# Two-layer hybrid trunk on one core: the attention bias loaded from POOL's queue, the weighted sums' finish marked urgent, and two tiles of the output projection in a pair of PSUM banks

## The chip, the cores and the metric

The kernel runs on one core of a Trainium2 chip. The metric is the device time of one execution in microseconds (us). Before the change it is 1185.64 us, the median of three runs (1185.47 to 1185.81).

## The reference

The program is a two-layer trunk over 256 latent tokens and 256 context tokens of width 1024. Each layer has a gated feed-forward block, a mixer and a second feed-forward block, each behind an RMS norm that is scaled and shifted by vectors made from the conditioning. Layer 0's mixer holds the code in question. It is an attention with 8 heads of 64, beside four pooling groups, and one output projection over both:

```python
q, k, v, u = jnp.split(hl @ w_in, [NA_WIDTH, 2 * NA_WIDTH, 3 * NA_WIDTH], axis=-1)
...
bias = rpb[:, ri[:, None, :, None], ci[None, :, None, :]]
s_win = jnp.einsum('brqhd,brkwhd->bhrqkw', qg, k_blk) * scale + bias
s_win = jnp.where(col_ok[:, None, :], s_win, NEG_INF)
...
p = jax.nn.softmax(jnp.concatenate([s_win, s_ctx], axis=-1), axis=-1)
o = einsum(p_win, v_blk) + einsum(p[..., n_win:], v_ctx)
...
pool = multiscale_pool(u, pool_w, pool_scale)
y_lat = jnp.concatenate([att, pool], axis=-1) @ w_out
```

So a query sees the keys of its grid window, with a bias out of a small table and a mask on the columns, and all context keys. Layer 1's mixer is a short gated convolution that ends in an output projection of the same form, `W_out(B * conv3(C * x_in))`.

## The kernel before

**Data.** Every weight and activation is split into a high and a low part, and a product is made of three matmuls (`mm3`, L250) or of two (`mm2`, L256), whose first takes high and low of the activation side by side as 512 columns. Weights come from memory in order of use as one stream (`Stream`, L66): SP loads a `raw` tile of two chunks (L90), ACT makes the high part `whi` (L102), DVE the low part `wlo` (L103). Three chunks are split ahead of use, in four buffers.

**Order.** The tile framework schedules the first stage by hand and the rest by its own planner, which takes instructions by priority (`tc.high_priority(offset=URGENT)` raises it) and fixes one order for each engine. On the chip every engine goes through its order without overtaking. SP, and POOL too, are such queues: an instruction that waits, a DMA issue as well, holds up all that stands behind it.

**PSUM.** There are two kinds of buffers: three pairs of banks (`pair`, L135) and two single banks (`single`, L138). A new pair takes the place of the one that was handed out three pairs before, and waits for that one's last reader; a single, of the one two singles before.

**The mixer of layer 0** (`even_mixer`, L627) goes through four turns i, each for two heads. A turn has: `v_turn` (L737), where TensorE (PE) turns the values over (`pvt`); `scores` (L746), where PE makes scores `ps`, `top` (L762) adds the bias to them on DVE (`sm`, L766) and takes the maximum (`st`, L771), and `power` (L773) makes the exponential on ACT (L776); then, for the next turn, the projections of queries, keys and values (`pq`, `pk`, `pv`) with their finishing steps `tq`, `tk`, `tv` on DVE, which read PSUM and so free its banks; `turn` (L782), the transposes of the probabilities `pT`; `weigh` (L794), the weighted sums `po`; and `weigh_finish` (L808), whose four steps on ACT and DVE write the result into `m2` (`mh`, `ml`). Ahead of the turns come the projections for the pooling groups, `pu`, read by DVE (`tu`, L611) and written to `u` (L669). POOL makes the running means `s`, `pd` out of `u` (`pool_means`, L674), and `pool_map` (L692) multiplies them in turn 1 (`pp`, L695, finished on ACT and DVE, L699 and L700).

**The bias.** `load_bias(i)` (L640) fills a tile of 128x1024 elements from the table by 8 DMAs of 64 KB, each 64 partitions by 4 rows of 64 elements. There are two buffers, so the load for turn i+2 waits until turn i's scores have read theirs. `bias_mask` (L652) then puts a large negative number at the masked columns, on DVE (L654). Before the change SP issues these DMAs, in one queue with the weights.

**The output projection** (`OutProj`, L898) makes eight tiles d of 128 output columns, each of eight blocks k. For layer 0 tiles 0 to 3 are begun early, without block 3, which is the last to be ready; `rest` (L921) adds that block to them and then makes tiles 4 to 7 whole, each in a single bank. Layer 1 has three early tiles, and 3 to 7 are made whole. Each finished tile goes to `residual` (L600; two steps on DVE at L603, for both halves of its 512 columns) and to the next norm's `feed` (L360; ACT L368 and L372, DVE L369 and L374).

Of the kernel before, what the change touches and what calls it, by code (L numbers as in the profile page):

```python
# [9 lines left out]
F32 = mybir.dt.float32  # L10
# [4 lines left out]
ALU = mybir.AluOpType  # L15
# [14 lines left out]
GW = 64  # L30
# [6 lines left out]
URGENT = 400  # L37
# [82 lines left out]
def hybrid_trunk_kernel(ctx: ExitStack, tc: tile.TileContext, xc, cols_d, modw, wst, poolw_d,  # L120
                        rpb, notok_d, rcnt_d, out):
    nc = tc.nc
# [12 lines left out]
    def pair(name):  # L135
        return ps2.tile([P, 2, 512], F32, tag="pair", name=name)

    def single(name):  # L138
        return ps1.tile([P, 512], F32, tag="single", name=name)
# [487 lines left out]
    def even_mixer(act):  # L627
        with tc.tile_pool(name="mix", bufs=2) as ap_:
            m2 = ap_.tile([P, KD, 2, T], F32R, name="m2", bufs=1)
            mh, ml = m2[:, :, 0, :], m2[:, :, 1, :]  # L630
# [9 lines left out]
            def load_bias(i):  # L640
                b = ap_.tile([P, 2, 2, 4, GW], F32, tag="bias", name=f"bias{i}")
                for r in range(4):
                    for h in range(2):
                        src = bass.AP(
                            rpb.tensor,
                            rpb.offset + (2 * i + h) * RPB_R * RPB_C + (7 - r) * RPB_C - 48,
                            [[1, GW], [RPB_C, 4], [1, GW]],
                        )
                        nc.sync.dma_start(b[(r % 2) * GW : (r % 2) * GW + GW, r // 2, h], src)
                return b  # L650

            def bias_mask(b):  # L652
# [155 lines left out]
            def weigh_finish(i, pt):  # L808
                t = ap_.tile([P, 544], F32, tag="t", name=f"to{i}", bufs=2)
                o, r = t[:, 0:256], t[:, 256:512]  # L810
                nc.scalar.copy(r, pt[:, 1, 0:256])
                nc.vector.tensor_tensor(o, pt[:, 0, 0:256], r, ALU.mult)
                nc.scalar.copy(mh[:, i, :], o)
                nc.vector.tensor_tensor(ml[:, i, :], o, mh[:, i, :].bitcast(F32), ALU.subtract)


            wq, wk = W.get(), W.get()
# [8 lines left out]
            held["v", 0] = [pv0[:, q, 0:258] for q in range(2)]  # L826
            rr.root()
            bias = {0: load_bias(0)}
            project_u(0)
            rr.spread()  # L830
# [17 lines left out]
            for i in range(4):  # L848
                v = v_turn(i)
                if i + 1 < 4:  # L850
                    bias[i + 1] = load_bias(i + 1)
                pr, top, power, parts = scores(i, bias[i])
                if i + 1 < 4:
# [17 lines left out]
                    po = weigh(i, tn, v, parts)  # L871
                    v_finish(i + 1)
                    weigh_finish(i, po)
                    bias_mask(bias[i + 1])
                    if i == 1:
                        pool_map()
                else:
# [13 lines left out]
                    proj_out.early(2)  # L891
                    po = weigh(i, tn, v, parts)
                    weigh_finish(i, po)
                    proj_out.early(3)
                    proj_out.rest()
            return a2

    class OutProj:  # L898
# [22 lines left out]
        def rest(self):  # L921
            for d in range(self.n):
                self.block(d, self.late, False, True)
                self.done(d)
            for d in range(self.n, KD):
                self.pts[d] = single(f"pwo{self.l}{d}")
                for k in range(KD):
                    self.block(d, k, k == 0, k == KD - 1)
                self.done(d)
# [136 lines left out]
    with tc.tile_pool(name="g1", bufs=1) as gp:  # L1066
# [6 lines left out]
        for a, b in ((0, 1), (1, 2), (2, 4), (4, 6), (6, 8)):  # L1073
            o = done[:, a:b, :]
# [128 lines left out]
```

## Time and profile before

The profiled execution took 1185.92 us, 0.28 us above the median; its first to its last instruction span 1184.1 us.

| what | us |
|---|---|
| median of the runs | 1185.64 |
| profiled execution | 1185.92 |
| its span | 1184.1 |
| PE busy (97% of the span) | 1154.5 |
| DVE busy (78%) | 928.4 |
| ACT busy (48%) | 573.9 |
| POOL busy (2%) | 21.1 |

How to read it: PE is the engine that is nearly always at work; the clock granted to it is 0.99 of full speed on the mean. A stretch in which another engine idles means little. What counts is an instruction for which PE waits, and then what that instruction had waited for. A row of a timeline has the start, the duration, the engine, the line, the operation, its output and inputs, the count, and in brackets the idle time ahead of it with what ended it. The mixer of layer 0 lies between 393 and 520 us of the span.

### The profile page before, as it was taken

How to read it: one execution, taken by the hardware profiler on the slowest of the kernel's cores; microseconds unless marked ns; L12 is line 12 of the kernel's file. 1: busy time of each engine (PE TensorE's matmuls, PEld its weight loads, DVE VectorE, ACT ScalarE, POOL GpSimd, SP SyncE). 2: the span in 40 equal slices, each digit the busy share in tenths (PEclk: the TensorE clock that was granted, in tenths of full speed). 3: DMA queues.
4: the chain of work that ended last, by engine and by line, in shares of the span. 5: the costliest groups of instructions: out<-in, count | busy, mean ns of one | idle time of the engine just before them, and what ended most of it. 6: DMA issues, size and time to landing. Idle time of an engine off the chain costs nothing.

```text
span 1184.1 us, 16775 instructions
## 1 busy us (share of the span) xinstructions
PE 1154.5 (97%) x6570; PEld 990.4 (84%) x6570; DVE 928.4 (78%) x1486; ACT 573.9 (48%) x890; POOL 21.1 (2%) x23
## 2 busy tenths in 40 slices
PE   4999999999999999999999999999999999999997
PEld 2568888888888987889888889888889989988886
DVE  8977686577788586788898998788998888766663
ACT  4353221223234445567556447555546656655642
POOL 2000000000000040000000000000000000000000
PEclk7999999999999999999999999999999999999998
DMA  7764455467676753245677985677895465555551
GB/s 274 255 221 156 179 191 185 143 217 275 241 272 238 230 136 90 76 165 187 242 264 271 342 316 205 221 271 260 314 336 188 149 213 174 183 181 191 198 179 36
DMA packets 45791, 250.54 MB, mean 212 GB/s; under 512 B 12944, under 2 KB 13328, under 8 KB 17552
## 3 DMA queue, kind: packets, MB, share of 16 engines
q1 hardware_dynamic: 45712, 249.48, 60.4%
q8 instruction: 51, 0.84, 0.3%
q14 instruction: 28, 0.23, 0.1%
HBM read 248.41 MB, written 1.05 MB: 211 GB/s over the span
## 4 chain that ended last, share of the span: by engine, by line
PE 93%; DVE 2%; DMA 1%; SPq 1%; ACT 1%; issue 1%; DVEq 0%; ACTq 0%
PE pf L260 13%; PE pz L260 10%; PE pf L261 8%; PE pa L253 6%; PE pa L254 6%; PE pa L252 6%; PE pz L261 5%; PE p L562 4%; PE py L253 3%; PE py L254 3%; PE py L252 3%; PE pf L253 3%; PE pf L252 3%; PE pf L254 3%; PE pwo L260 2%; PE pf L263 2%
## 5 line engine op out<-in xcount | busy, mean ns | idle before, releaser
L102 ACT CAST whi<-raw 128x1024 fp32r<-128x1024 f32 x312 | 327.8, 1051 | 394.2 <-PE pa L253 114.1
L103 DVE TENSOR_TENSOR wlo<-raw,whi 128x1024 fp32r<-128x1024 f32 x312 | 382.0, 1225 | 150.6 <-ACT whi L102 149.9
L260 PE MATMUL pf<-al,whi 128*128 128x512 f32 x672 | 241.0, 397 | 0.0
L203 DVE CUSTOM_DVE_ANT_0 jk<-mr,cvec,cols 128x1024 bf16<-128x1024 f32 x184 | 236.5, 1285 | 1.6
L261 PE MATMUL pf<-al,wlo 128*128 128x256 f32 x768 | 199.9, 281 | 0.0
L260 PE MATMUL pz<-g,whi 128*128 128x512 f32 x504 | 178.6, 398 | 0.0
L261 PEld LDWEIGHTS pf<-al,wlo 128*128 128x128 f32 x768 | 145.0, 189 | 8.9
L260 PEld LDWEIGHTS pf<-al,whi 128*128 128x128 f32 x672 | 126.4, 188 | 26.2
L261 PE MATMUL pz<-g,wlo 128*128 128x256 f32 x528 | 144.3, 281 | 0.0
L260 PEld LDWEIGHTS pz<-g,whi 128*128 128x128 f32 x504 | 94.7, 188 | 22.1
L252 PE MATMUL pa<-xh,whi 128*128 128x512 f32 x288 | 112.0, 389 | 0.0
L253 PE MATMUL pa<-xl,whi 128*128 128x512 f32 x288 | 112.0, 389 | 0.0
L254 PE MATMUL pa<-xh,wlo 128*128 128x512 f32 x288 | 112.0, 389 | 0.0
L261 PEld LDWEIGHTS pz<-g,wlo 128*128 128x128 f32 x528 | 99.7, 189 | 2.3
L253 PE MATMUL pf<-ah,whi 128*128 128x258 f32 x288 | 81.6, 283 | 0.0
L252 PE MATMUL pf<-ah,whi 128*128 128x258 f32 x288 | 80.9, 281 | 0.0
L254 PE MATMUL pf<-ah,wlo 128*128 128x258 f32 x288 | 80.8, 281 | 0.0
L252 PE MATMUL py<-gh,whi 128*128 128x512 f32 x176 | 68.5, 389 | 0.0
L253 PE MATMUL py<-gl,whi 128*128 128x512 f32 x176 | 68.5, 389 | 0.0
L254 PE MATMUL py<-gh,wlo 128*128 128x512 f32 x176 | 68.5, 389 | 0.0
L619 ACT COPY tf<-pf 128x512 f32<-128x512 f32 x48 | 28.2, 587 | 73.4 <-PE pf L263 73.4
L252 PEld LDWEIGHTS pa<-xh,whi 128*128 128x128 f32 x288 | 54.1, 188 | 11.3
(257 smaller groups left out, 1915.7 us busy)
## 6 DMA issues: line engine op xcount, KB each, us to landing
raw<-in_wst SPq DMA_DIRECT2D x156, 1024.0 KB, 5.0
mr<-in_modw SPq DMA_DIRECT2D x64, 1024.0 KB, 5.0
mr<-in_modw SPq DMA_DIRECT2D x16, 512.0 KB, 5.0
raw<-in_wst SPq DMA_DIRECT2D x8, 512.0 KB, 6.5
bias<-in_rpb SPq DMA_DIRECT2D x32, 64.0 KB, 5.8
xl_all<-in_xc SPq DMA_DIRECT2D x2, 512.0 KB, 6.7
xc_all<-in_xc SPq DMA_DIRECT2D x2, 512.0 KB, 8.1
out<-done SPq DMA_DIRECT2D x3, 256.0 KB, 2.6
```

What stands on the lines that cost most here:

```text
L102: nc.scalar.copy(hi, src)
L103: self.last = nc.vector.tensor_tensor(lo, src, hi.bitcast(F32), ALU.subtract).ins
L203: nc.vector.tensor_tensor_reduce(out=junk, in0=raw[:, h, :], in1=cvec[:, q, :], scale=1.0, scalar=cols[:, b : b + 1], op0=ALU.mult, op1=AL ...
L252: nc.tensor.matmul(out, wh, xh, start=first, stop=False)
L253: nc.tensor.matmul(out, wh, xl, start=False, stop=False)
L254: nc.tensor.matmul(out, wl, xh, start=False, stop=last)
L260: nc.tensor.matmul(out, wh, both, start=first, stop=False)
L261: nc.tensor.matmul(out[:, 0:256], wl, x[:, 0, :], start=False, stop=False)
L263: nc.tensor.matmul(out, wh, both, start=False, stop=True)
L562: nc.tensor.matmul(pts[j], wf[:, j * P : j * P + P], f32, start=first, stop=last)
L619: nc.scalar.copy(t, pt[:, :, 256:512])
```

## The change

There are three edits.

- `load_bias` issues its DMAs from POOL's queue (`nc.gpsimd.dma_start`) and no longer from SP's.
- the four steps of `weigh_finish` are put under `tc.high_priority(offset=URGENT)`.
- in `OutProj.rest` the first two whole tiles (4 and 5 in layer 0; 3 and 4 in layer 1) are put into the two banks of one new pair; the others stay in single banks.

```diff
@@ load_bias
-                        nc.sync.dma_start(b[(r % 2) * GW : (r % 2) * GW + GW, r // 2, h], src)
+                        nc.gpsimd.dma_start(b[(r % 2) * GW : (r % 2) * GW + GW, r // 2, h], src)
@@ weigh_finish
-                nc.scalar.copy(r, pt[:, 1, 0:256])
-                nc.vector.tensor_tensor(o, pt[:, 0, 0:256], r, ALU.mult)
-                nc.scalar.copy(mh[:, i, :], o)
-                nc.vector.tensor_tensor(ml[:, i, :], o, mh[:, i, :].bitcast(F32), ALU.subtract)
+                with tc.high_priority(offset=URGENT):
+                    nc.scalar.copy(r, pt[:, 1, 0:256])
+                    nc.vector.tensor_tensor(o, pt[:, 0, 0:256], r, ALU.mult)
+                    nc.scalar.copy(mh[:, i, :], o)
+                    nc.vector.tensor_tensor(ml[:, i, :], o, mh[:, i, :].bitcast(F32), ALU.subtract)
@@ OutProj.rest
             for d in range(self.n, KD):
-                self.pts[d] = single(f"pwo{self.l}{d}")
+                if d == self.n:
+                    free = pair(f"pwo{self.l}{d}")
+                self.pts[d] = free[:, d - self.n, :] if d < self.n + 2 else single(f"pwo{self.l}{d}")
                 for k in range(KD):
```

The planner makes a new order out of this. The numbers behind names are buffers: `bias_2955`, `bias_3130`, `bias_3372` and `bias_3630` are the bias of turns 0, 1, 2 and 3.

POOL's queue at the start of the mixer, and where the pooling means end (the difference; + is new):

```order
 L461 TENSOR_TENSOR sq_191<-sq_191 128x256
 L632 MEMSET u 128x1088
+L649 DMA bias_2955<-in_rpb 64x4x64 x8
+L649 DMA bias_3130<-in_rpb 64x4x64 x8
 L676 TENSOR_TENSOR pd<-u 128x256
 L676 TENSOR_TENSOR s_3110<-u 128x3x271
...
 L688 TENSOR_TENSOR pd<-pd,rc 128x1024
 L689 TENSOR_TENSOR pd<-pd,u 128x1024
+L649 DMA bias_3372<-in_rpb 64x4x64 x8
+L649 DMA bias_3630<-in_rpb 64x4x64 x8
```

The loads for turns 0 and 1 stand ahead of the pooling means, those for turns 2 and 3 behind them.

DVE's order at the start of the mixer, from the norm's last step to the first pooling group (`tq`, `tk`, `tv` of turn 0, `tu` of the first group):

```order
 L103 TENSOR_TENSOR wlo_2901<-raw_2621,whi_2900 128x1024
+L654 COPY_PREDICATED bias_2955<-notok,neg 128x1024
 L613 TENSOR_TENSOR tq_3029<-pq_2819,rs_97 128x258
 L611 TENSOR_TENSOR tk_3033<-pk_2820,rs_97 128x516
...
 L103 TENSOR_TENSOR wlo_2966<-raw_2706,whi_2965 128x1024
+L654 COPY_PREDICATED bias_3130<-notok,neg 128x1024
 L103 TENSOR_TENSOR wlo_2996<-raw_2706,whi_2995 128x1024
-L654 COPY_PREDICATED bias_2955<-notok,neg 128x1024
 L611 TENSOR_TENSOR tu_3102<-pu_2964,rs_97 128x516
```

The mask of turn 0 moved ahead of `tq`, and the mask of turn 1, which stood in turn 0 behind the scores, moved ahead of `tu`.

DVE's order in turn 0 where the values of turn 1 are finished (`th`: the turned probabilities):

```order
 L792 COPY th_3264<-pT_3265 128x4x128
 L792 COPY th_3274<-pT_3275 128x4x128
+L654 COPY_PREDICATED bias_3372<-notok,neg 128x1024
 L729 TENSOR_TENSOR tv_3354<-pv_3293,rs_97 128x258
-L654 COPY_PREDICATED bias_3372<-notok,neg 128x1024
 L731 TENSOR_SCALAR tv_3354<-tv_3354 128x256
```

The mask of turn 2 moved by one place, ahead of the first step of `tv`. The mask of turn 3 keeps its place ahead of `tv` in turn 1. On ACT and DVE the steps of `weigh_finish` stand between the same neighbours as before.

PE's order in layer 0's output projection. Before (`pwo_3974` is the pair of tiles 2 and 3, `pwo_4063` tile 4, `pwo_4093` tile 5; `pf` is the next block):

```order
L261 MATMUL pwo_3974<-m_2800,wlo_3914 128x256
L263 MATMUL pwo_3974<-m_2800,whi_3913 128x512
L260 MATMUL pwo_4063<-m_2800,whi_3934 128x512
...
L261 MATMUL pwo_4063<-m_2800,wlo_3935 128x256 x2
L263 MATMUL pwo_4063<-m_2800,whi_3934 128x512
L260 MATMUL pwo_4093<-m_2800,whi_3981 128x512
```

And with the change (`pwo_4063` is the new pair, `pwo_4120` tile 6, `pwo_4150` tile 7):

```order
L260 MATMUL pwo_4063<-m_2800,whi_3934 128x512
...
L261 MATMUL pwo_4063<-m_2800,wlo_3935 128x256 x2
L263 MATMUL pwo_4063<-m_2800,whi_3934 128x512
L260 MATMUL pwo_4120<-m_2800,whi_4017 128x512
...
L260 MATMUL pwo_4150<-m_2800,whi_4066 128x512
L252 MATMUL pf_4204<-ah_3888,whi_4093 128x258
L253 MATMUL pf_4204<-ah_3888,whi_4093 128x258
L260 MATMUL pwo_4063<-m_2800,whi_3981 128x512
```

Tile 5, the pair's second half, now comes after tile 6. In layer 1 tile 4, the second half there, comes after tile 5 and inside tile 6.

## The prediction

> **What bounds the kernel now.** I read the page first, then the waits of PE, then the timeline of the mixer engine by engine.
>
> ```profile
> span 1184.1 us, 16775 instructions
> PE 1154.5 (97%) x6570; PEld 990.4 (84%) x6570; DVE 928.4 (78%) x1486; ACT 573.9 (48%) x890; POOL 21.1 (2%) x23
> ```
>
> PE works 97% of the span, so only an instruction for which PE stops counts. In PE's waits three rows belong to code that the change touches:
>
> ```profile
> PE pwo L260 <- DVE xl_all L603: 2.4, 3, 1.1
> PE pvt L741 <- DVE m L700: 1.9, 1, 1.9
> PE pvt L741 <- DVE tv L731: 0.6, 2, 0.3
> ```
>
> That is 4.9 us in all, 0.4% of the time: no edit here can gain more than that. Where they lie, in PE's timeline:
>
> ```profile
> 442.51 0.44 PE L741 MATMUL pvt<-ident,tv 128*128 128x128 f32 x2 [0.28 <-DVE tv L731]
> 468.33 0.66 PE L741 MATMUL pvt<-ident,tv 128*128 128x128 f32 x4 [1.87 <-DVE m L700]
> 507.26 0.47 PE L260 MATMUL pwo<-m,whi 128*128 128x512 f32 x1 [1.13 <-DVE xl_all L603]
> 972.49 0.47 PE L260 MATMUL pwo<-y,whi 128*128 128x512 f32 x1 [1.12 <-DVE xl_all L603]
> ```
>
> The first two end behind masks of the bias. These are the loads of the bias on SP's queue, and DVE's masks:
>
> ```profile
> 448.22 5.23 SPq L649 DMA_DIRECT2D bias<-in_rpb  x8
> 440.10 1.40 DVE L654 COPY_PREDICATED_SCALAR bias<-notok,neg 128x1024 f32 x1 [3.07 <-DMA bias<-in_rpb]
> 461.62 1.41 DVE L654 COPY_PREDICATED_SCALAR bias<-notok,neg 128x1024 f32 x1 [4.44 <-issue]
> ```
>
> The eight loads for turn 3 begin at 448.22 and their mask starts at 461.62, after 4.44 us of idle DVE. The order has that mask wait for its loads alone, so I read the 13.4 us as their price from first issue to mask. DVE was late by it, the pooling map was drained late behind it (L700), and PE lost 1.87 us at 468.33. So the bias's loads decide already, and they are what the change moves.
>
> **The change, part by part.**
>
> *The precedence of the weighted sums.* The order on ACT and DVE has the four steps between the same neighbours as before. Price: nothing.
>
> *SP without the bias.* SP's weight loads no longer stand behind the bias's. No split waited for a load:
>
> ```profile
> DVE wlo L103 <- ACT whi L102: 149.9, 165, 5.3
> ```
>
> DVE's splits wait for ACT, and ACT for PE's release of a buffer. Gain: nothing, and what hides it, three chunks split ahead, stays.
>
> *The loads on POOL's queue.* Here the sum lies. No row shows a DMA issued from POOL. What is nearest:
>
> ```profile
> L649 SPq DMA_DIRECT2D bias<-in_rpb x32: 595/615/3187, 397.7 to 452.8; - x32
> DMA to landing us min/median/max: 3.7/5.8/9.5
> ```
>
> Let d be the time that each further load adds, and 3.7 us the shortest landing. From below, eight loads take 8 x 0.595 + 3.7 = 8.5 us. From above, POOL's own instructions are the only measure: 21.1 us for 23 are 0.9 us each, the longest issue was 3.19 us, and their geometric middle is d = 1.7, eight loads 17.3 us. For the forecast I take the row of the same eight loads, 13.4 us, so d = (13.4 - 3.7) / 8 = 1.2. Most of that is not the issue (0.6 us) but the transfer of rows of 256 B, which stays the same transfer.
>
> The Trainium skill, "DMA: Bandwidth & Descriptors", under "Latency and other measured facts" and "Anatomy of one DMA — SWDGE (gpsimd) path", gives about 1 us to the first byte for a DMA issued from GpSimd, and per DMA 2.0 us plus its bytes at 436 GB/s. By it eight loads would be about 8 x 1 + 2.15 = 10.2 us, an estimate, and the sum below would be +2.8 us instead of +13.4; no run here shows it yet.
>
> POOL's queue is empty at the start of the mixer and then is not:
>
> ```profile
> 396.52 1.00 POOL L632 MEMSET u<- 128x1088 f32 x1 [380.41 <-ACT sq L334]
> 422.13 2.46 POOL L676 TENSOR_TENSOR s<-u 128x813 f32<-128x813 f32 x1 [3.89 <-DVE u L669]
> 431.82 2.38 POOL L689 TENSOR_TENSOR pd<-pd,u 128x1024 f32<-128x1024 f32 x1
> ```
>
> Place 1: the first sixteen loads start at 397.5 where the memset ends. Turn 0's have landed at 397.5 + 13.4 = 410.9, turn 1's 8 x 1.2 later, at T1 = 420.5. Their masks now stand ahead of `tq` and `tu`. Queued behind them on DVE are these:
>
> ```profile
> 406.08 0.43 DVE L613 TENSOR_TENSOR tq<-pq,rs 128x258 f32<-128x258 f32 x1 [0.77 <-ACT rs L298]
> 414.12 1.42 DVE L654 COPY_PREDICATED_SCALAR bias<-notok,neg 128x1024 f32 x1
> 415.44 0.67 DVE L611 TENSOR_TENSOR tu<-pu,rs 128x516 f32<-128x516 f32 x1
> 416.03 1.21 DVE L103 TENSOR_TENSOR wlo<-raw,whi 128x1024 fp32r<-128x1024 f32 x1
> 417.16 0.60 DVE L669 TENSOR_SCALAR u<-tu 128x256 f32<-128x256 f32 x2
> 420.70 0.69 DVE L611 TENSOR_TENSOR tu<-pu,rs 128x516 f32<-128x516 f32 x1 [0.67 <-PE pu L254]
> 421.43 0.62 DVE L669 TENSOR_SCALAR u<-tu 128x256 f32<-128x256 f32 x2
> 421.96 1.22 DVE L103 TENSOR_TENSOR wlo<-raw,whi 128x1024 fp32r<-128x1024 f32 x1
> 423.75 0.76 DVE L766 SCALAR_TENSOR_TENSOR sm<-ps,bias 128x256 f32<-128x256 f32 x2 [0.56 <-ACT sm L764]
> 429.29 0.19 ACT L776 ACTIVATION_READ_ACCUMULATOR sm<-sm,st 128x1 f32 x1
> 431.68 0.49 PE L787 MATMUL pT<-ident,sm 128*128 128x128 f32 x3
> ```
>
> Start to start (the rows overlap by 0.1 us), turn 1's mask is 1.3, four splits 1.1 each, two `tu` 0.6 and 0.7, four steps of `u` 0.3 each: from T1 to `sm` 8.2 us, so `sm` starts at 428.7 and not 423.75, 5.0 late. Its chain ended at 429.5 in the exponential, and PE needed it at 431.68: 2.2 of slack. PE stops for 2.8 us. Turn 0's mask, from 410.9, holds `tk`, which frees a pair, until about 413.3. PE needs that pair for the second `pu`, its 49th matmul of this name:
>
> ```profile
> 414.69 0.29 PE L252 MATMUL pu<-ah,whi 128*128 128x258 f32 x1
> ```
>
> So turn 0's mask costs nothing.
>
> Place 2: `u` is complete 7.1 us behind T1, at 427.6 and not 422.05. POOL then needs the 12.1 us that lie between 422.1 and 434.2, so it ends at 439.7, and only then issues the loads for turn 2. They land at 439.7 + 13.4 = 453.1, where the mask starts, against 440.10 before. Behind the mask on DVE are `tv`'s four steps; PE waits for `tv` to turn the values over and everything on PE stands behind that. Before, the second half of `pvt` came 442.51 - 440.10 = 2.4 us after the mask's start. Now one more step of `tv` lies between:
>
> ```profile
> 436.61 0.41 DVE L729 TENSOR_TENSOR tv<-pv,rs 128x258 f32<-128x258 f32 x1
> ```
>
> With 0.35 for it that is 2.75 us: `pvt` at 455.9, 13.4 us late in all, the 2.8 us of place 1 included. This is the main term.
>
> Place 3: turn 3's loads wait, as before, until turn 1's scores have read the buffer; POOL's queue is free by then (439.7 + 8 x 1.2 = 449.3, against 448.2 + 13.4). With 13.4 us again the mask comes as late as it did, and the 1.87 us stay. With 11.5 us or less they would go.
>
> *The pair of banks.* The waits of 1.13 and 1.12 us are for `residual` to free a single bank; the pair's old reader, a copy of the turned probabilities, stands ahead of the weighted sums. Gain -2.25 us, the lower end. But the order puts the second half behind the next tile: its first matmul waits for the first half's residual. Its weights then hold their buffer for a tile longer, and the split that takes this buffer stands on DVE behind more residual steps. Counting these steps by rows like those above (a residual 0.45, a split 1.1), I get PE waiting up to 2.5 us in each layer for `wlo` of the next block: +2.75 in all with the gain off, the upper end. I take 0, between the ends; the two nearest rows, the waits themselves, are as large as what may come.
>
> Sum: 2.8 + 10.6 + 0 + 0 = +13.4 us on 1185.92 for the profiled execution, 1199.3; on the median, 1199.0.
>
> **The rivals.** *No cost:* POOL issues as cheaply as SP and the transfer is shorter with nothing queued ahead. With 8.5 us for eight loads T1 is 397.5 + 16 x 0.595 + 3.7 = 410.7 and place 1 costs nothing; turn 2's mask is at 434.2 + 8.5 = 442.7, `pvt` 2.9 us late; turn 3's mask comes 4.9 earlier, -1.87. That is +1.0, with the banks' ends from 1184.4 to 1189.4 on the median. For it: the shortest landing was 3.7 us. Against it: the eight loads whose mask the trace shows took 13.4.
>
> *Faster:* a quicker load on POOL's queue moves turn 2's mask no later than it was. This decides from 440.10 - 434.2 = 5.9 us for eight loads; below it the 1.87 us go, and with the banks' 2.25 the median is 1181.5. Against it: eight issues at 0.595 alone are 4.8 us, and the shortest landing is 3.7.
>
> *Starved:* POOL's loads stand still while DVE holds SBUF, and DVE is busy for 12.3 us (third figure of busy time) of these 20:
>
> ```profile
> 400.00:420.00 20.00, 20.00 (x169) 20.00 (x169) 12.31 (x18) 9.43 (x12) 0.66 (x1) 1.00 0.70 187
> ```
>
> If d rises to the longest issue, 3.19 us, eight take 29.2 us: T1 = 452.2, 34.5 us lost at place 1, `pvt` 61 us late, turn 3's mask 15.8 later: about 1262. From d = 1.7 on, which the same sums make 1215 (10.7 at place 1, 14.4 at place 2, 3.9 at place 3), I count it as this rival. The Trainium skill, "SBUF — State Buffer", in "SBUF: two separate sides", warns of just this: descriptors of a DMA from GpSimd can't be written while a two-port operation of VectorE holds the shared port. By that rule little would come of it here, since of the rows quoted at place 1 only the steps of `u` copy from SBUF to SBUF with one input.
>
> *The change doesn't do what it says:* the precedence moves nothing, which the order shows, and the pair isn't free for its second tile. That makes the banks' part a loss of up to 2.75 us; it lies inside the range and doesn't turn the sign.
>
> **How the numbers follow.** About 0.2%, 2.4 us, is what a measurement of this kernel can tell from no change. The forecast, a loss at turn 2's mask with d from 0.75 to 1.7, has 0.72; no cost 0.13; faster 0.06; starved 0.09. The likeliest time is 1199.0. The range goes from 1185, the lower end of the no-cost case with the banks half gained, to 1215 at d = 1.7. Slower by over 0.2% takes the forecast and the starved case, 0.81; same is the no-cost case, 0.13; faster 0.06.
>
> **What would show it.** Right: in the profile after, `pvt` of turn 1 waits 8 us or more for `tv`, ahead of it DVE's mask of turn 2 waits for the bias's DMA, and the issues of that DMA on POOL start behind `pd` L689; at 420 us a mask is waited for too. The rows on `pwo` with 1.1 us are gone, others on `pwo` or `pf` waiting for `wlo` have come. Wrong: POOL's issue rows at 0.6 us or less with masks that don't idle DVE; a `pvt` no later than 443 us; or a loss whose waits lie in the output projection.

## The result, and the profile after

The changed kernel takes 1192.51 us (median of four runs, 1192.31 to 1195.24) against 1185.68 us for the kernel before beside it: ratio 1.0053, 95% interval 1.0039 to 1.0067. A second series gave 1192.17 against 1185.68 us, ratio 1.0050 (1.0037 to 1.0062). So it is slower, as forecast, but by 6.8 us and not by 13.4.

The first trace of the changed kernel is of its slowest execution, 1195.24 us. That of the second series is of one at 1192.17 us, near the median; the account below is made with it, and called the second trace. These are PE's waits in the first, with the total, the number of times and the longest:

```profile
PE pvt L741 <- DVE tv L731: 8.9, 1, 8.9
PE pu L252 <- DVE tk L611: 1.0, 1, 1.0
PE pvt L741 <- DVE m L700: 0.4, 1, 0.4
PE pf L254 <- DVE wlo L103: 0.2, 1, 0.2
```

The waits of 1.1 us on `pwo` are gone. The wait of 1.9 us behind `m` (L700) has shrunk to 0.4, and one of 8.9 us for `tv` has come. In the second trace PE stands like this at the value transpose of turn 1 (with the scores `ps` that follow it), DVE at the masks of turns 1, 2 and 3, and POOL at the end of the pooling means:

```profile
450.54 1.41 PE L741 MATMUL pvt<-ident,tv 128*128 128x128 f32 x4 [8.75 <-DVE tv L731]
451.88 3.42 PE L755 MATMUL ps<-kh,qh 64*128 64x512 f32 x8
```

```profile
417.93 1.43 DVE L654 COPY_PREDICATED_SCALAR bias<-notok,neg 128x1024 f32 x1 [0.53 <-DMA bias<-in_rpb]
448.44 1.35 DVE L654 COPY_PREDICATED_SCALAR bias<-notok,neg 128x1024 f32 x1 [10.59 <-DMA bias<-in_rpb]
469.10 1.44 DVE L654 COPY_PREDICATED_SCALAR bias<-notok,neg 128x1024 f32 x1 [1.47 <-DMA bias<-in_rpb]
```

```profile
425.76 2.45 POOL L676 TENSOR_TENSOR s<-u 128x813 f32<-128x813 f32 x1 [2.62 <-DVE u L669]
435.45 3.46 POOL L689 TENSOR_TENSOR pd<-pd,u 128x1024 f32<-128x1024 f32 x1
438.85 4.89 POOL L649 DMA_DIRECT2D bias<-in_rpb  x8
458.92 4.86 POOL L649 DMA_DIRECT2D bias<-in_rpb  x8 [15.18 <-DVE sm L766]
```

This is place 2 of the prediction: POOL issues turn 2's loads the moment the means are done, at 438.85. DVE idles 10.59 us in front of the mask, and PE 8.75 us for `tv` behind it. A load of eight DMAs costs POOL 4.89 us, 0.61 each, as on SP (0.615).

The transpose itself takes 1.41 us for four, and the scores 3.42, where before they took 0.88 and 1.99. The reason stands in the column PEclk (third from the end; 1.00 is full speed) of these stretches of the second trace:

```profile
443.00:444.00 1.00, 0.00 (x0) 0.00 (x0) 0.00 (x0) 0.00 (x0) 0.74 (x2) 1.00 0.69 41
444.00:445.00 1.00, 0.00 (x0) 0.00 (x0) 0.00 (x0) 0.00 (x0) 0.00 (x0) 0.78 0.91 90
445.00:446.00 1.00, 0.00 (x0) 0.00 (x0) 0.00 (x0) 0.00 (x0) 0.00 (x0) 0.50 0.88 66
453.00:454.00 1.00, 1.00 (x6) 0.49 (x4) 0.42 (x1) 0.11 (x1) 0.00 (x0) 0.50 1.02 131
454.00:455.00 1.00, 1.00 (x4) 0.09 (x2) 0.00 (x0) 0.00 (x0) 0.00 (x0) 0.60 0.72 295
455.00:456.00 1.00, 1.00 (x8) 0.78 (x7) 0.00 (x0) 0.67 (x3) 0.00 (x0) 1.00 0.98 418
```

PE stops at 441.8. From 444.6 the granted clock is 0.50, and it stays there until 454.8, 4.3 us after PE has begun again. In the first trace it is 0.50 from 448.8 to 459.0, as long, but with 6.7 us of it beside PE's work.

How far PE is behind the kernel before, at the start of the same step:

| start of | before | second trace | later by | first trace, later by |
|---|---|---|---|---|
| `pq`, turn 0 | 393.25 | 393.58 | 0.33 | 0.66 |
| `pT`, turn 0 (place 1 lies ahead) | 431.68 | 432.02 | 0.34 | 1.93 |
| `pvt`, turn 1 (place 2) | 441.78 | 450.54 | 8.76 | 10.52 |
| `pk` for turn 2, after the slow clock | 447.78 | 458.23 | 10.45 | 13.30 |
| `pwo`, layer 0 (place 3 lies ahead) | 490.93 | 499.75 | 8.82 | 11.69 |
| norm after layer 0's mixer half (`pn`) | 712.27 | 719.85 | 7.58 | 10.44 |
| end of the span | 1184.1 | 1190.4 | 6.3 | 9.4 |

By differences, for the second trace: 0.3 that was there ahead of the mixer, 0.0 at place 1, +8.4 at place 2, +1.7 in the stretch of the slow clock, -1.6 between there and the output projection (place 3), -1.2 and -1.3 in the two output projections. For the first: 0.7, +1.3, +8.6, +2.8, -1.6, -1.2, -1.0.

The 1.7 and 2.8 are differences to the kernel before, where the transposes came in two halves and the stretch from `pvt` to `pk` took 6.0 us. Where all four came at once and the clock stayed full it took 5.4 and 5.5 us (two of the runs below). So the slow clock by itself cost 2.2 and 3.3 us, of which 0.5 was made up by the undivided transposes.

### The profile page after: what moved, and what is told of

Read it like the earlier page. It is cut to its first block, busy times and chain, and to the rows that moved or that the text cites. A ratio compares the mean times of both kernels' runs of the same rounds, so it can differ in the third digit from the quotient of the medians.

```text
span 1193.5 us, 16785 instructions
## 1 busy us (share of the span) xinstructions
PE 1158.0 (97%) x6570; PEld 992.3 (83%) x6570; DVE 926.9 (78%) x1486; ACT 573.1 (48%) x890; POOL 42.6 (4%) x55
## 2 busy tenths in 40 slices
DMA packets 38112, 250.55 MB, mean 210 GB/s; under 512 B 4752, under 2 KB 5136, under 8 KB 9872
## 3 DMA queue, kind: packets, MB, share of 16 engines
q0 software_dynamic: 1024, 2.10, 2.2%
## 4 chain that ended last, share of the span: by engine, by line
PE 61%; issue 32%; POOL 2%; DMA 2%; DVE 1%; ACT 0%; DVEq 0%; POOLq 0%; ACTq 0%
PE pf L260 13%; PE pz L260 10%; PE pf L261 8%; PE pz L261 5%; PE pf L253 3%; PE pf L254 3%; PE pf L252 3%; PE pwo L260 2%; PE pf L263 2%; DMA bias<-in_rpb 2%; PE pwo L261 1%; PE pc L260 1%; POOL bias L649 1%; PE pc L253 1%; PE pc L252 1%
## 5 line engine op out<-in xcount | busy, mean ns | idle before, releaser
L254 PEld LDWEIGHTS pa<-xh,wlo 128*128 128x128 f32 x288 | 54.1, 188 | 11.2
```

What stands on the lines that cost most here:

```text
L254: nc.tensor.matmul(out, wl, xh, start=False, stop=last)
```

## The experiments

The theory made from these traces: the loss is turn 2's load behind the pooling means, met by a mask that stands ahead of `tv`, with the clock's fall on top; the banks gain, the precedence does nothing. The rivals: loads from POOL's queue are dear wherever they stand; the masks ahead of `tq` and `tu` are a good part; the clock falls for another reason. Four runs share each chip: the first four have 1186.19 us for the kernel before, the next four 1186.24, the last four 1185.68.

### The precedence alone

Only the `with tc.high_priority(offset=URGENT)` around the four steps of `weigh_finish`.

> The kernel before with the precedence alone. Theory A (the loss is the wait for turn 2's bias behind the pooling means; the precedence does nothing, the banks gain 2.3 us): 1185.7 us, ratio 1.000, within 0.3 us. Rival (the precedence pushes the mask or the finishing steps of the values aside): over 1187 us.

Measured: 1185.69 us, ratio 0.9993 (0.9984 to 1.0002). It does nothing.

### The pair of banks alone

```diff
-                self.pts[d] = single(f"pwo{self.l}{d}")
+                if d == self.n:
+                    free = pair(f"pwo{self.l}{d}")
+                self.pts[d] = free[:, d - self.n, :] if d < self.n + 2 else single(f"pwo{self.l}{d}")
```

> The kernel before with the pair of banks alone. Theory A: both waits of 1.1 us for the residual go and the second half waits for nothing, so 1183.4 us (1185.7 less 1.26 and 1.07), ratio 0.998. Rival (the weights that the second half holds make PE wait for the next split, so that the pair is no gain by itself): 1185.7 us or more.

Measured: 1183.05 us, ratio 0.9970 (0.9959 to 0.9982), a little more than expected. The waits on `pwo` are gone, and what came for the second half is 0.2 us:

```profile
PE pf L254 <- DVE wlo L103: 0.2, 1, 0.2
```

So the weights that the second half holds for a tile longer cost almost nothing, and the gain is at least the two waits.

### The loads on POOL's queue alone

```diff
-                        nc.sync.dma_start(b[(r % 2) * GW : (r % 2) * GW + GW, r // 2, h], src)
+                        nc.gpsimd.dma_start(b[(r % 2) * GW : (r % 2) * GW + GW, r // 2, h], src)
```

> The kernel before with the bias's loads on POOL's queue alone; single banks and no precedence. Theory A: what the change costs without its gain, 1192.5 + 2.3 = 1194.8 us, ratio 1.008, with the value transpose of turn 1 waiting 8 to 10 us for the finished values behind the mask of turn 2. Rival (a good part of the loss comes from the three edits together): 1191 us or less.

Measured: 1194.26 us, ratio 1.0062 (1.0049 to 1.0074). `pvt` waits 8.2 us for `tv`, both waits of 1.1 us on `pwo` are there. The whole loss belongs to this edit. In this trace `pu` and `pT` of turn 0 lie as far apart as before (22.74 us in both): place 1 costs nothing.

### PE kept busy during the stop, 60 products

Behind the weighted sums of turn 0, in the changed kernel (this adds work that the reference has not; `pt[:, 0, 256:384]` is read by nobody):

```diff
+                if i == 0:
+                    for j in range(60):
+                        nc.tensor.matmul(pt[:, 0, 256:384], ident, ident, start=True, stop=True)
```

> The changed kernel with 60 products of the identity with itself behind the weighted sums of turn 0, into a part of the bank that nobody reads, so that PE works through most of the wait for turn 2's bias. They are no part of the reference's computation. If the stop of PE is what takes the TensorE clock down to half (theory A), the granted clock stays near 1.0 there, the wait itself stays and the time is about 2.8 us below that of the changed kernel's profiled execution, 1192.4 us; the median of 1192.5 may then be of executions in which the clock fell less or not at all, and stays. If the clock fell for another reason, it falls here too, and its scores take 3.7 us again instead of 1.9 us.

Measured: 1195.13 us, ratio 1.0064 (1.0052 to 1.0077). The clock stays at 1.00 throughout, and `ps` takes 1.99 us. But 60 products last 13.66 us, and `tv` was ready 5.4 us before their end: the dose was too large, and its cost ate the gain.

### The same with 36 products

> As with 60 products of the identity, but 36, since 60 lasted 13.3 us and so 5.4 us longer than the wait. 36 take 8 us and end about where the finished values come. If the stop is what halves the clock, the granted clock stays at 1.0, the scores of turn 1 take 1.9 us, and the time is 1.6 to 2.8 us (what the halved clock cost in the two traces that have it) below that of the changed kernel: 1189.7 to 1191 us. If the halved clock costs nothing in the end, 1192.5 us.

```profile
442.16 8.30 PE L808 MATMUL po<-ident 128*128 128x128 f32 x72
451.81 0.44 PE L741 MATMUL pvt<-ident,tv 128*128 128x128 f32 x2 [1.35 <-DVE tv L731]
452.91 1.99 PE L755 MATMUL ps<-kh,qh 64*128 64x512 f32 x8
```

Measured: 1191.54 us, ratio 1.0047 (1.0035 to 1.0060). In the trace (PE's timeline, above) the scores take 1.99 us again, and from `pvt` to `pk` it is 6.0 us, as before the change, where the second trace of the changed kernel has 7.7 and the first 8.8. So it is the stop that halves the clock, and against the kernel before that costs 1.7 to 2.8 us. The times alone do not show it: the interval overlaps with that of the changed kernel. In the execution traced the mask of turn 2 came 10.15 us behind its first issue and not 9.6, which took back a part.

### The pooling means behind turn 2's loads

In the changed kernel, `load_bias(2)` and the means go into turn 0, behind `power(1)`. `gate_u` is one step on POOL that multiplies turn 0's last maximum by the zeros at the edge of `u` and writes them back, and so holds POOL until that maximum is there (the heart of the edit; the call of `pool_means` in its old place goes):

```diff
+                    if i == 0:
+                        bias[2] = load_bias(2)
+                        gate_u()
+                        pd = pool_means()
```

> The changed kernel, but POOL makes the pooling means only behind the loads for turn 2 (a small step on POOL that reads the last maximum of turn 0 holds them back; it adds zeros and changes nothing that is computed). Theory A (the loss is the wait for turn 2's bias because its loads stand behind the means): the stop of 8 to 9 us at the value transpose of turn 1 goes and with it the fall of the clock; what stays of the change is the 2.3 us of the banks, the 1.9 us of turn 3's mask that is no longer late, and 0 to 1.3 us lost at the first masks: 1181.5 to 1183.5 us, below the kernel before. Rival (loads from POOL's queue are dear by themselves, or take DVE's port, wherever they stand): 1188 us or more, with masks that still wait for their loads.

Measured: 1188.32 us, ratio 1.0011 (1.0002 to 1.0020). This missed the theory's 1181.5 to 1183.5 and fell where the rival had put it. The trace says why. POOL, DVE, PE around the end of turn 0:

```profile
429.97 4.86 POOL L649 DMA_DIRECT2D bias<-in_rpb  x8 [16.11 <-DVE sm L771]
444.49 2.34 POOL L689 TENSOR_TENSOR pd<-pd,u 128x1024 f32<-128x1024 f32 x1
```

```profile
443.21 1.37 DVE L654 COPY_PREDICATED_SCALAR bias<-notok,neg 128x1024 f32 x1 [3.62 <-DMA bias<-in_rpb]
444.46 0.42 DVE L733 TENSOR_TENSOR tv<-pv,rs 128x258 f32<-128x258 f32 x1
444.92 2.06 DVE L735 TENSOR_SCALAR tv<-tv 128x256 f32<-128x256 f32 x1
```

```profile
447.03 1.41 PE L745 MATMUL pvt<-ident,tv 128*128 128x128 f32 x4 [4.56 <-DVE tv L735]
```

Three things: the loads wait for turn 0's scores to read the buffer, so they start at 429.97 at best; they now take 13.2 us to the mask, because a weight load of 1 MB runs among them (258, 385 and 328 GB/s from 437 to 440, where turn 2's bias alone moves at most some 100); and `tv`'s step of 0.35 us takes 2.06, ending 0.15 us after POOL's last mean. The stop is halved, not gone, and the clock falls here too (`ps` 3.79 us). The experiment had moved the means onto the place that it was to clear. That the load on POOL is dear by itself, the rival's reason, is decided by the runs below.

### Turns 0 and 1 on SP, 2 and 3 on POOL, means behind the loads, pair of banks

> The kernel before with the pair of banks; turns 0 and 1 of the bias on SP's queue as before, turns 2 and 3 on POOL's, the pooling means behind turn 2's loads. Theory A: 1185.7 less 2.3 for the banks, less 1.9 and 0.3 for the two waits at the value transposes, 1181.2 us, ratio 0.996. Rival as in the run with the means behind the loads: 1185 us or more.

Measured: 1186.46 us, ratio 0.9995 (0.9985 to 1.0005): missed for the same reasons. DVE and POOL here:

```profile
440.59 1.41 DVE L654 COPY_PREDICATED_SCALAR bias<-notok,neg 128x1024 f32 x1 [3.35 <-DMA bias<-in_rpb]
442.33 2.33 DVE L735 TENSOR_SCALAR tv<-tv 128x256 f32<-128x256 f32 x1
```

```profile
427.32 5.01 POOL L649 DMA_DIRECT2D bias<-in_rpb  x8 [29.13 <-DMA bias<-in_rpb]
442.18 2.34 POOL L689 TENSOR_TENSOR pd<-pd,u 128x1024 f32<-128x1024 f32 x1
```

Turn 2's loads start at 427.32 and their mask 13.3 us later, no sooner than from SP before (440.10). `tv` again ends 0.14 us behind POOL's step, PE waits 2.6 us, and the clock falls for 3.4 us. Three of the eleven executions took 1183.5 to 1183.8 us, the others 1185.9 to 1187.7. The trace is of one at 1186.79, so what the three had otherwise stays open.

### Turns 2 and 3 back on SP

In the changed kernel `(nc.gpsimd if i < 2 else nc.sync).dma_start(...)`.

> The changed kernel, but the loads for turns 2 and 3 issued by SP again, those for turns 0 and 1 by POOL. Theory A: the stop at turn 1's value transpose is gone, the one of 1.9 us at turn 3's mask is back, the banks keep their gain, the first masks cost 0 to 1.3 us: 1183.4 to 1185 us. Rival (the first masks, which now stand ahead of the finishing of queries and keys, are a good part of the loss): 1187 us or more.

Measured: 1187.10 us, ratio 1.0005 (0.9994 to 1.0015). The 8.8 us are gone, but not all. SP's issues and PE:

```profile
428.31 3.13 SPq L649 DMA_DIRECT2D bias<-in_rpb  x4
431.56 0.53 SPq L90 DMA_DIRECT2D raw<-in_wst  x1
432.13 4.81 SPq L649 DMA_DIRECT2D bias<-in_rpb  x4
```

```profile
443.11 0.44 PE L741 MATMUL pvt<-ident,tv 128*128 128x128 f32 x2 [1.93 <-DVE tv L731]
444.45 3.20 PE L755 MATMUL ps<-kh,qh 64*128 64x512 f32 x8
```

The first masks still stand ahead of `tq` and `tu`, so turn 0's scores free the buffer late: the loads start at 428.31, the mask at 441.48, PE waits 1.9 us, and this stop too brings a half clock (443.5 to 446.9). The rival is right in this: the first masks count, not by a stop of PE at their place, but through the buffer that turn 2's loads need.

### The masks behind the scores, loads on POOL

The changed kernel as it is, but the number that a mask writes is made from the last maximum of the turn before, so that the planner can't put it ahead of `tv`:

```diff
+                    nc.vector.scalar_tensor_tensor(ng[:, 0, :], held["st"], 0.0, neg[:, 0, :], ALU.mult, ALU.add)
                 nc.vector.copy_predicated(
-                    bf, notok.to_broadcast([P, 16, GW]), neg.to_broadcast([P, 16, GW])
+                    bf, notok.to_broadcast([P, 16, GW]), ng.to_broadcast([P, 16, GW])
```

> The changed kernel, its loads all on POOL and behind the means as they are, but the masks of turns 1, 2 and 3 stand behind the maxima of the turn before (the mask's number is made in one step of one column from the last maximum, times zero, so that what is computed stays the same). So the mask of turn 2 no longer stands ahead of the finished values, for which PE waits. Theory A (the loss is that place in DVE's order, met by a late load): both waits at the value transposes and the fall of the clock go, the banks keep their gain: the time of the kernel before less 2.8, 1.9 and 0.3, plus 0 to 0.4 at the first masks: about 1181 us, ratio 0.996. Rival (a load from POOL's queue costs by itself, through DVE's port or the weights' transfers): ratio over 1.000.

Measured: 1181.73 us, ratio 0.9966 (0.9952 to 0.9979), on one chip with the changed kernel's 1192.17. DVE's mask of turn 2, and PE at the place of the stop:

```profile
449.79 1.42 DVE L658 COPY_PREDICATED_SCALAR bias<-notok,ng 128x1024 f32 x1
```

```profile
441.13 0.66 PE L745 MATMUL pvt<-ident,tv 128*128 128x128 f32 x4
441.72 1.99 PE L759 MATMUL ps<-kh,qh 64*128 64x512 f32 x8
```

The means still stand ahead of turn 2's loads, and these still come from POOL. Only the masks of turns 1 to 3 have another place, and the stop and the slow clock are gone: 10.4 us (the wait of 0.42 us behind `m` in turn 3 is there as before). A part of that is not turn 2's mask: with turn 1's no longer ahead of `tu` the loads start at 435.43 and not 438.85, 2.3 us sooner when the 1.1 us by which this trace is ahead at `pq` are taken off. But by the 9.6 us of the second trace even these would be in only at about 445, 4 us behind the start of `pvt` here, so the mask's place decides. The load was late for the mask's place, not for its use: turn 2's scores read the bias only behind 464. So the rival of a dear queue falls.

### The masks behind the scores, loads on SP

> The same place of the masks, in the kernel before with the pair of banks: all loads on SP's queue. Theory A: it is the masks' place and not the queue that counts, so the same time as with POOL's queue, ratio 0.996, within 0.5 us of it. Rival (POOL's queue frees SP's and so the weights): slower than with POOL's queue by 1 us or more.

Measured: 1181.54 us, ratio 0.9958 (0.9945 to 0.9970). So the two queues can't be told apart by the time, as expected.

### Only turn 3 on POOL

The kernel before, the pair of banks, and `(nc.gpsimd if i == 3 else nc.sync).dma_start(...)`.

> The kernel before with the pair of banks and only turn 3's loads on POOL's queue, which by then is free. Theory A: turn 3's mask comes by 10 us behind its first issue instead of 13.4, the wait of 1.9 us goes, the rest is the run with the pair alone: ratio 0.996, about 1181.3 us. Rival (the weight load that stretched the eight loads on SP's queue stretches them on POOL's as well): the 1.9 us stay, ratio 0.9975.

Measured: 1181.52 us, ratio 0.9963 (0.9950 to 0.9975). POOL and DVE:

```profile
448.01 5.06 POOL L649 DMA_DIRECT2D bias<-in_rpb  x8 [14.56 <-DVE sm L766]
```

```profile
460.02 1.42 DVE L654 COPY_PREDICATED_SCALAR bias<-notok,neg 128x1024 f32 x1 [3.31 <-DMA bias<-in_rpb]
```

The mask comes 12.0 us behind the first issue, so the wait behind `m` goes from 1.9 to 0.9 us and not to 0.4. The expectation's 10 us did not hold with a weight load at its end (295 and 418 GB/s from 458 to 460).

### The changed kernel again

> The changed kernel once more, beside the next three on one chip: ratio 1.0053 to 1.0065, about 1192.5 to 1193.5 us.

Measured: 1192.17 us, ratio 1.0050 (1.0037 to 1.0062), a little under what was expected. The pair alone is faster than both kernels, and three versions are faster still, at 1181.5 to 1181.7 us with intervals that overlap. The simplest of them is the one with turn 3 on POOL.

## Why the prediction was right in direction and wrong in size

The step that failed is the price of eight loads in place 2: 13.4 us in the sum, 9.6 in the traces. The slow clock, which the sum had at nothing, made up a part of it.

*The place and the mechanism* were right: `pvt` of turn 1 waits 8.75 us for `tv`, ahead of it the mask of turn 2 waits for its DMA, whose issues start behind `pd` L689; taking the masks from their places removes all of it. The chain up to POOL was near as well: `s` at 427.6 by the sum, 427.54 in the first trace and 425.76 in the second; POOL free at 439.7 by the sum, 440.63 in the first and 438.85 in the second. That is luck in part: the first sixteen loads took 20.1 us in the second trace and not 23.0, and POOL's means took 13.1 us and not 12.1 (the last one 3.46 us and not 2.38, beside a split of DVE at the same time).

*Place 2, the price of eight loads.* I took 13.4 us from the same eight loads on SP and said that most of it was the transfer "which stays the same transfer". But a weight load was part of the 13.4 us. These are the stretches of the kernel before, with the share of the DMA engines and GB/s at the end:

```profile
448.00:450.00 2.00, 2.00 (x19) 2.00 (x18) 2.00 (x5) 2.00 (x5) 0.00 (x0) 1.00 0.06 6
450.00:452.00 2.00, 2.00 (x19) 2.00 (x18) 1.50 (x2) 1.31 (x4) 0.00 (x0) 1.00 0.52 64
452.00:454.00 2.00, 2.00 (x20) 2.00 (x18) 1.33 (x2) 0.36 (x1) 0.00 (x0) 1.00 0.54 49
454.00:456.00 2.00, 2.00 (x20) 2.00 (x19) 1.97 (x4) 2.00 (x4) 0.00 (x0) 1.00 0.59 64
456.00:458.00 2.00, 2.00 (x19) 2.00 (x18) 1.18 (x2) 0.10 (x1) 0.00 (x0) 1.00 0.73 62
458.00:460.00 2.00, 2.00 (x20) 2.00 (x19) 0.00 (x0) 0.00 (x0) 0.00 (x0) 1.00 0.72 111
460.00:462.00 2.00, 2.00 (x19) 1.69 (x19) 0.38 (x1) 0.84 (x1) 0.00 (x0) 1.00 0.88 353
```

Up to 458 these are (6 + 64 + 49 + 64 + 62) x 2 = 490 KB, and the eight loads are 524 KB. So nearly all of the bias had been moved in 10 us; then the weights came, 1 MB at up to 353 GB/s, and the mask started only at 461.62. The profile names no cause for DVE's wait there, but the trace has every packet: the last of the bias ended at 461.12. SP had issued the weights at 456.01. These are the packets, MB and share of the 16 DMA engines from 448 to 458 and from 458 to 459:

```profile
q1 hardware_dynamic: 2028, 0.49, 48.8%
q1 hardware_dynamic: 76, 0.02, 76.3%
```

A packet kept an engine busy for 0.04 us in the first stretch and for 0.16 in the second. So the tail of the bias was slowed just as the weights came. In the changed kernel PE stands still while turn 2's loads run, and no weights are among them:

```profile
442.00:444.00 2.00, 0.00 (x0) 0.00 (x0) 0.00 (x0) 0.25 (x1) 1.74 (x3) 1.00 1.15 68
446.00:448.00 2.00, 0.00 (x0) 0.00 (x0) 0.00 (x0) 0.00 (x0) 0.00 (x0) 0.50 0.41 66
```

From first issue to mask, in turns 2 and 3 wherever DVE waited for it and their queue issued the eight in one go: 9.4 to 10.5 us without a weight load or with one only at the very end (twelve times, all from POOL), 12.0 with one in the last two microseconds (POOL), 13.1 to 13.4 with more of one (six times: four from SP, two from POOL). With weights beside them both queues took the same; eight loads from SP without weights are in no trace. (Where SP issued a weight load between them, in turn 2, it was 13.2 to 14.2.) That the weights are the cause rests on these nineteen and on the packets above, not on a run that removes them alone. The packets also were not the same transfer: 256 B each on SP's queue, 2 KB on POOL's.

In the second trace `pvt` starts 8.8 us late, 8.4 of them at this place, where the sum had 13.4. The difference is 3.8 us of price (13.4 less 9.6) and 0.9 us by which POOL was free sooner than in the sum.

*Place 1*: +2.8 forecast, 0.0 and 1.3 measured. In the total it made no difference, because `pvt` waits for DVE's chain and that holds whatever PE has lost before. `sm` was late as forecast (428.51 in the first trace against 428.7), but the slack was mis-read: I counted from the last exponential, while PE's first transposes need only those of the first head, which before ended at 426.7, 5 us ahead of `pT`. What the first trace did lose there came through turn 0's mask, which I had at nothing: its loads took 15.9 us, it held `tk`, and PE waited 1.0 us for the pair.

*The clock* was not in the sum at all: +1.7 and +2.8 us. These stops of PE had a price behind their end.

*Place 3* was taken at 0 on the same 13.4 us, and the text said that the 1.87 us would go with 11.5 or less. It was 10.2: -1.4 us at the wait itself.

*The pair of banks* was taken at 0 between -2.25 and +2.75: it is the lower end, -2.2 to -2.5 in the traces of the changed kernel. The counted wait for `wlo` was 0.2 us and not 2.5: the order of the steps was right, but the splits ran far enough ahead.

The two steps at nothing, *the precedence* and *SP without the bias*, were right. Added up for the second trace: 13.4 less 5.0 (place 2, 8.4 in place of 13.4), less 1.4 to 1.6 (place 3), less 2.5 (banks), plus 1.7 (clock) and 0.3 from ahead of the mixer are 6.3 to 6.5, against the span's 6.3. So three terms that I had too dear stand against one that I did not know; the total fell into the range, the size was double.

Why the small price would not have given the right sum either: POOL's queue at the first sixteen loads, second trace.

```profile
397.81 5.01 POOL L649 DMA_DIRECT2D bias<-in_rpb  x8
405.13 1.22 POOL L649 DMA_DIRECT2D bias<-in_rpb  x2 [2.31 <-DMA bias<-in_rpb]
```

From the ninth on POOL waits until the earlier ones have landed, so sixteen loads took 20.1 us (397.81 to the mask at 417.93), two full prices and not one and eight small steps. That made `u`, the means and turn 2's loads late even at 10 us for eight. The Trainium skill, "DMA: Bandwidth & Descriptors", "Anatomy of one DMA — SWDGE (gpsimd) path", by which I had estimated 10.2 us for eight loads, agrees with the traces on that price (9.6 us in the second). Its parts do not fit, so the agreement is partly luck: an issue took 0.61 us and not 1, and a load landed 3.6 us behind its issue at the earliest. The sum by it, +2.8, lacked this wait and the clock; it also left out that its own price makes turn 1's mask late (T1 = 415.65, `u` complete at 422.75 and not 422.05), with which it is +3.4.

## What to carry to other kernels

Before you ask which queue should load a tile, ask where the instruction that waits for it stands in its engine's order, and whether it must stand there: here the places of the masks were worth 10 us, the queue nothing that the times show (1181.73 and 1181.54 us). A duration from first issue to use holds what else the DMA engines did in it, so compare only stretches with the same neighbours. When a change makes PE stop, look at the granted clock behind the stop before adding up: in this kernel stops of 1.9 us and more were followed by half a clock.

## What the runs showed of the hardware

*The clock falls after short stops.* PE stops of 1.93, 2.61, 4.56, 8.20, 8.75 and 8.93 us in this place were followed by scores of 3.2 to 3.8 us in place of 1.99; after stops of 1.87 us or less (turn 3 of the kernel before) the matmuls kept their speed, and with PE kept at work as well. By PEclk the half clock lasted 3.4 us for the stops of 1.93 and 2.61 us, 6.8 for 4.56 and 10.2 for the three of over 8: one, two and three times 3.4. From `pvt` to `pk` it cost 1.5 to 3.3 us against the same stretch at full clock. The Trainium skill, "TensorE: Matmul & The Clock Gate", Part 1, has half rate after at least one idle window of about 3.4 us that runs freely; that the moment varies agrees with the traces (the clock fell 0.4 us behind the end of the stop of 1.93 us, but 5.4 us into that of 8.93), and so does a step of 3.4 us; that a whole idle window is needed does not: 1.93 us did it.

*DVE and POOL hold each other up.* `tv`'s step from SBUF to SBUF took 2.06 and 2.33 us, not 0.35, each time ending 0.14 or 0.15 us behind a step of POOL of 2.34 us. The Trainium skill, "SBUF — State Buffer", in "SBUF: two separate sides", has one port pair that the first of the two holds for its whole instruction; the rows agree. That POOL's DMA issues would be held up in the same way is not to be seen: their median was 0.615 to 0.624 us in the traces, the longest 0.78 us.

*POOL's queue moves larger pieces.* The bias was 1024 packets for 2.10 MB in POOL's queue, 2 KB each, and the kernel's packets under 512 B fell from 12944 to 4752, by 8192, which at 256 B each are the same 2.10 MB; yet eight loads beside a weight load took the same 13 us on both.
